# A hybrid decoder layer on one core: the products with x by a 2x2 recursion of seven products, ahead of everything else

## The chip, the cores and the metric

The kernel runs on one core of a Trainium2 chip. The metric is device time of one execution in microseconds (us). The engines named below are TensorE (PE in the profile; its weight loads are shown as PEld), VectorE (DVE), ScalarE (ACT), GpSimd (POOL) and SyncE (SP), whose queue issues all transfers.

## The reference

One decoder layer is applied to a prompt of 1024 tokens and to eight decode tokens, which have caches of their own. Both groups share the weights; the kernel puts them side by side as T = 1032 columns. D is 1024. Everything is float32.

```python
z = x @ w_in                                # [T, 7680], the single combined projection
xr, yr, q, k, v, xq, g = jnp.split(z, SPLIT_IDX, axis=-1)   # 1024, 1024, 1024, 256, 256, 1024, 3*1024
xc, conv_new = causal_conv(xr, conv_buf, conv_w, conv_b)    # width 4
hs, h_new = rg_lru(xc, h0, ...)             # h_t = a_t h_(t-1) + u_t; a, u from two block-diagonal products
a_out = hs * gelu(yr)
s_out = swa_prompt(q, k, v, sinks)          # window 128, 16 query heads, 4 key heads of 64; swa_decode for decode tokens
c_out = mem_attn(xq, mem_k, mem_v)          # 256 memory tokens, 4 heads of 256
gates = sigmoid(g + b_gates)                # three gates
merged = sum(gates[n] * (branch_n @ w_branch[n]))
h = layer_norm(ALPHA * x + merged @ w_out)
gt, up = split(h @ w_gate_up)               # 2 * 2816
h = layer_norm(ALPHA * h + (silu(gt) * up) @ w_down)
```

The prompt's memory keys and values come from `mem_prompt @ w_mem_kv`; the decode tokens read theirs from caches (`cmk`, `cmvT`), and local keys and values too (`cwk`, `cwvT`). New cache contents and states are outputs as well.

## The kernel before

Activations lie transposed: features on 128 partitions, tokens along the row. The 1032 tokens are cut into chunks of 384, 384 and 264 (`CH`). A product of two float32 matrices is made of three single-pass products: each operand is split into a high and a low part (`split`: ACT writes the rounded copy, L58, and DVE subtracts it, L59), and `mm3` (L79) adds high×high, high×low and low×high in PSUM (L84 to L86). A tile of 128 output features (`mm_tile`, L88) runs over eight blocks of the contraction for each chunk, so it is 72 matmuls. Weights come by `weights` (L72): one transfer of 512 KB into one of two raw buffers and a split. `load_branch` (L97) brings a branch's output back from DRAM and splits it.

The framework fixes one order of instructions for each engine ahead of time, so each engine works strictly in order and a waiting instruction holds up all that stand behind it on its engine. All transfers are issued by SP in one queue. `issue_after` puts a piece of work behind a given instruction in that order.

The stages in order:

1. `mem_attention` (L242). x is loaded and split into resident operands. For each of four heads: the query products of two feature tiles (`xq`), the memory's keys and values (`mem_kv`, L155: `mk`, `mv`), then scores, softmax, transposes and the weighted sum (`mem_head`, L202: `cs`, `cp`, `cpt`, `co`), whose result goes to DRAM. `dec_mem` (L578) does the decode tokens' attention into their own memories on DVE: query rows go through DRAM and are broadcast (`dcq`), keys come by two buffers (`dck`), DVE multiplies and adds up (`dcj`, L593), PE transposes the scores (`dct`), and the same follows with values (`dcv`, `dcpb`, `dcw`, L616).
2. `win_attention` (L406). Value products (`win_kv`), key products (`win_keys`), query products (`win_queries`) and 32 blocks of local attention (`win_block`, L350), 4 key heads by 8 blocks of 128 queries. A block has score matmuls (`bs`), a masked maximum (L371), exponentials (L377), a normalization that is shared by DVE (L386) and POOL (L384), transposes with a split (`bt`, `bph`, `bpl`), the product with the values (`bo`) and the sum of its two halves (L402). The products for the next key head stand between blocks.
3. `lru` (L541). For each of eight feature tiles the product `xr`, the convolution, the gate products, the recurrence (a scan on DVE, L524) and, from `yr`, the gelu; the result stays in SBUF as split operands.
4. `merge` (L706). For branch a, then c, then s: gate products (`ga`, `gc`, `gs`) two tiles ahead, and branch products (`bra`, `brc`, `brs`). The decode tokens' local attention (`dec_win`, scores with `dsk`, `dsq`, `dsj`, L655; softmax; values with `dsv`, `dspb`, `dsw`, L700) is put one token at a time behind these products.
5. `out_proj` and `ffn` (L893, L930) with the two layer norms.

So 58 feature tiles of x @ w_in and the values (216 matmuls with 256 columns) are spread over stages 1 to 4.

Of the kernel before, what the change touches and what calls it, by code (L numbers as in the profile page):

```python
# [2 lines left out]

# [4 lines left out]
F32 = mybir.dt.float32  # L8
# [21 lines left out]
DEC_VALUES = ((), (), (), (0,1), (2,), (3,), (4, 5), (6, 7))  # L30
YR_AFTER = ((2,), (3,), (4,), (5,), (6,), (), (), (7,))
# [10 lines left out]
class Builder:  # L42
# [6 lines left out]
    # ---------------------------------------------------------------- helpers  # L49
    def slot(self, kind, c, name, n=None):  # L50
        return self.slots.tile([P, n or CH[c][1]], F32R, tag=f"{kind}{c}", name=name)
# [4 lines left out]
    def split(self, hi, lo, src):  # L56
        """hi + lo = src exactly, in the operand format of the tensor engine's single-pass float32."""
        ins = self.nc.scalar.copy(hi, src).ins  # L58
        self.nc.vector.tensor_sub(lo, src, hi.bitcast(F32))  # L59
        return ins  # L60
# [18 lines left out]
    def mm3(self, ps, terms, closes=True):  # L79
        """ps = sum over terms of stationary^T moving, each operand as (hi, lo)."""  # L80
        nc = self.nc
        last = len(terms) - 1
        for i, ((sh, sl), (mh, ml)) in enumerate(terms):
            nc.tensor.matmul(ps, sh, mh, start=i == 0, stop=False)  # L84
            nc.tensor.matmul(ps, sh, ml, start=False, stop=False)  # L85
            self.last_mm = nc.tensor.matmul(ps, sl, mh, start=False, stop=closes and i == last).ins  # L86

    def mm_tile(self, w, act, c, name, tag="mm", nk=KT):  # L88
        """[128 features, tokens of chunk c] = w^T act, w = (hi, lo) of an m-tile, act[k][c] = (hi, lo)."""
# [7 lines left out]
    def load_branch(self, src, name):  # L97
        """a branch's output from DRAM, [128, 8, T]: act[k][c] = (hi, lo)."""
# [10 lines left out]
    # ---------------------------------------------------------------- phases  # L109
    def setup(self):  # L110
        nc, ctx, tc, io = self.nc, self.ctx, self.tc, self.io
        self.cst = ctx.enter_context(tc.tile_pool(name="cst", bufs=1))
        self.slots = ctx.enter_context(tc.tile_pool(name="slots", bufs=16))
        self.wpool = ctx.enter_context(tc.tile_pool(name="wpool", bufs=3))
# [5 lines left out]
        self.mask = self.cst.tile([P, 256], F32, name="mask")  # L120
# [6 lines left out]
    def load_consts(self):  # L127
        nc, io = self.nc, self.io
        nc.sync.dma_start(self.vec, io["vec"])
        nc.sync.dma_start(self.ident, io["cst"][:, 0:P])  # L130
        nc.sync.dma_start(self.mask, io["cst"][:, P:P + 256])

    def load_x(self, c):
        """x of chunk c, staged through what will hold queries."""
        t0, n = CH[c]
        for k in range(0, KT, 2):
            raw = self.ph.tile([P, TP], F32, tag="cq", name=f"xr{k}_{c}", bufs=6)[:, :2 * n]
            raw = raw.rearrange("p (k t) -> p k t", k=2)
            self.x_loaded = self.nc.sync.dma_start(raw, self.io["xT"][:, k:k + 2, t0:t0 + n]).ins
            for j in range(2):  # L140
                hi, lo = self.slot("H", c, f"xh{k + j}_{c}"), self.slot("L", c, f"xl{k + j}_{c}")
                self.split(hi, lo, raw[:, j, :])
                self.x[k + j][c] = (hi, lo)

    def load_mem(self):
        nc, io = self.nc, self.io
        self.memx = []
        for k in range(KT):
            hi, lo = self.slot("H", 0, f"memh{k}", NM), self.slot("L", 0, f"meml{k}", NM)
# [5 lines left out]
    def mem_kv(self, h):  # L155
        """keys of head h by feature, values by memory token."""
        nc, io = self.nc, self.io
        mk, mv = [], []
        for m in (2 * h, 2 * h + 1):
# [8 lines left out]
            hi, lo = self.slot("H", 1, f"mkh{m}", NM), self.slot("L", 1, f"mkl{m}", NM)  # L168
# [3 lines left out]
        for tt in range(2):  # L172
# [9 lines left out]
            hi, lo = self.slot("H", 2, f"mvh{h}_{tt}", 256), self.slot("L", 2, f"mvl{h}_{tt}", 256)  # L182
# [3 lines left out]

    def dec_query(self, ps, qd, m, scale):
        """keeps the scaled query of the decode tokens, [128 features, 8]."""
        self.nc.scalar.mul(qd[:, m * NB:(m + 1) * NB], ps[:, 256:264], scale)

    def mem_query(self, w, q, m, c):
        t0, n = CH[c]
        ps = self.mm_tile(w, self.x, c, f"xq{m}_{c}")
        n = min(n, TP - t0)
        self.split_scaled(q[0][:, t0:t0 + n], q[1][:, t0:t0 + n], ps[:, :n], 1.0 / 16.0)
        if c == 2:
            self.dec_query(ps, self.qdc, m, 1.0 / 16.0)

    def mem_query_tiles(self, m):
        return tuple(self.ph.tile([P, TP], F32R, tag="cq", name=f"cq{e}{m}", bufs=6) for e in "hl")  # L200
# [41 lines left out]
    def mem_attention(self):  # L242
        nc, io = self.nc, self.io
        self.qdc = self.cst.tile([P, KT * NB], F32, name="qdc")
        self.x = [[None] * 3 for _ in range(KT)]
        w = [self.weights(io["win"][28], D, "wxq0")]
        self.load_x(0)
        w.append(self.weights(io["win"][29], D, "wxq1"))
        self.load_x(1)
        self.load_mem()  # L250
        self.load_x(2)
        with self.tc.issue_after(self.x_loaded):
            self.load_consts()
        q = [self.mem_query_tiles(m) for m in range(2)]
        for c in range(3):
            for m in range(2):
                self.mem_query(w[m], q[m], m, c)
        self.lru_consts()
        for h in range(4):
            mk, mv = self.mem_kv(h)  # L260
            self.mem_head(h, q, mk, mv)
            if h < 3:
                q = []
                for m in (2 * h + 2, 2 * h + 3):
                    w = self.weights(io["win"][28 + m], D, f"wxq{m}")
                    q.append(self.mem_query_tiles(m))
                    for c in range(3):
                        self.mem_query(w, q[-1], m, c)
            with self.tc.issue_after(self.x_loaded):
                self.dec_mem(h)  # L270
        nc.sync.dma_start(self.scr["c"][:, :, TP:T], self.cdec)

    def win_kv(self):
        """keys as stacks [hi; hi] and [lo; lo] per kv head, values as [hi | lo] per block."""
        nc, io = self.nc, self.io
        self.kd = self.cst.tile([P, 2 * NB], F32, name="kd")
        self.vd = self.cst.tile([NB, 256], F32, name="vd")
        self.vs = []
        w = [self.weights(io["wv"][j], D, f"wv{j}") for j in range(2)]
        for blk in range(9):  # L280
            c, off = min(blk // 3, 2), (blk - 3 * min(blk // 3, 2)) * P
            nt = P if blk < 8 else NB
            ps = self.bank("mm", f"v{blk}")[:nt, :256]
            self.mm3(ps, [
                ((self.x[k][c][0][:, off:off + nt], self.x[k][c][1][:, off:off + nt]),
                 (w[k // 4][0][:, (k % 4) * 256:(k % 4 + 1) * 256], w[k // 4][1][:, (k % 4) * 256:(k % 4 + 1) * 256]))
                for k in range(KT)
            ])
            if blk == 8:
                nc.scalar.copy(self.vd, ps)  # L290
                break
            if blk == 7:
                vraw = self.sm.tile([P, 256], F32, tag="kvraw", name="pwv", bufs=1)
                nc.scalar.copy(vraw, ps)
                nc.sync.dma_start(io["o_pwv"], vraw)
            pair = []
            for half in range(2):
                kind = "H" if blk % 2 == 0 else "L"
                v = self.slots.tile([P, 256], F32R, tag=f"{kind}{half}", name=f"vs{blk}_{half}")
                v3 = v.rearrange("p (g e d) -> p g e d", g=2, e=2)  # L300
                src = ps[:, half * P:(half + 1) * P].rearrange("p (g d) -> p g d", g=2)
                nc.scalar.copy(v3[:, :, 0, :], src)
                nc.vector.tensor_sub(v3[:, :, 1, :], src, v3[:, :, 0, :].bitcast(F32))
                pair.append(v)
            self.vs.append(pair)
        self.ks = {}

    def win_keys(self, m):
        nc, io = self.nc, self.io
        w = self.weights(io["win"][24 + m], D, f"wk{m}")  # L310
        kk = [[self.ph.tile([P, TP], F32R, tag="ks", name=f"ks{m}_{g}_{e}", bufs=5) for e in range(2)]
              for g in range(2)]
        for c, (t0, n) in enumerate(CH):
            ps = self.mm_tile(w, self.x, c, f"k{m}_{c}")
            n = min(n, TP - t0)
            for g in range(2):
                src = ps[g * 64:(g + 1) * 64, :n]
                own = kk[g][0][g * 64:(g + 1) * 64, t0:t0 + n]
                for e in range(2):
                    nc.scalar.copy(kk[g][0][e * 64:(e + 1) * 64, t0:t0 + n], src)  # L320
                for e in range(2):
                    nc.vector.tensor_sub(kk[g][1][e * 64:(e + 1) * 64, t0:t0 + n], src, own.bitcast(F32))
            if c == 2:
# [792 lines left out]
```

## Time and profile before

Three runs took 2108.48, 2110.21 and 2118.28 us: median 2110.21 us.

| | |
|---|---|
| profiled execution, time and span | 2110.1 us |
| PE busy | 2039.2 us (97%) |
| PE weight loads busy | 1992.5 us (94%) |
| DVE busy | 1067.1 us (51%) |
| ACT busy | 755.0 us (36%) |
| POOL busy | 99.0 us (5%) |
| moved by transfers | 166.90 MB, 79 GB/s over the span |

Busy time is the time in which an engine had an instruction under way; a matmul that waits for its clock or for its operand inside the pipeline counts as busy too. The granted clock is the TensorE clock as a share of full speed. In a group's row stand the count, the sum, the mean length of one in ns, and then the idle time of the engine just before them with what ended it.

### The profile page before, as it was taken

The page shows a single profiled execution, that of the slowest core. Times are in us where ns is not written, and L with a number is a line of the kernel's source. Part 1 is how long each engine was busy: PE and PEld are TensorE (multiplying, and loading weights), DVE is VectorE, ACT ScalarE, POOL GpSimd, SP SyncE. Part 2 cuts the span into 40 slices and gives each one's busy share as a digit, 9 for nine tenths or more (in the row PEclk, how much of TensorE's full clock was granted, in tenths as well). Part 3 has the DMA queues.
Part 4 walks back from the last instruction along what each step waited for, and adds up shares of the span by engine and source line. Part 5 has one row for each costly group of instructions (what it writes and reads, how often), then busy time and mean ns, then how long its engine had stood idle before and what let it go on. Part 6 is the DMA issues. An engine that isn't in the chain of part 4 may idle for free.

```text
span 2110.1 us, 32562 instructions
## 1 busy us (share of the span) xinstructions
PE 2039.2 (97%) x13013; PEld 1992.5 (94%) x13013; DVE 1067.1 (51%) x2434; ACT 755.0 (36%) x1574; POOL 99.0 (5%) x167
## 2 busy tenths in 40 slices
PE   8998889999999999999999999999999999999997
PEld 8988888889899999999999999899999999999996
DVE  6455569998777643423442257832322322223357
ACT  6333347777766521311131144522201221112134
POOL 0000001111211100000000001200000000000001
PEclk9999999999999999999999999999999999999999
DMA  6366641112111122422441123011111111111112
GB/s 228 128 188 196 185 121 41 47 36 56 46 43 46 48 94 81 154 78 88 126 131 41 50 85 101 17 60 41 50 50 41 51 50 44 47 42 59 38 53 81
DMA packets 100855, 166.90 MB, mean 79 GB/s; under 512 B 12112, under 2 KB 69696, under 8 KB 100672
## 3 DMA queue, kind: packets, MB, share of 16 engines
q1 hardware_dynamic: 100704, 164.82, 24.9%
q8 instruction: 102, 1.67, 0.3%
q14 instruction: 49, 0.40, 0.1%
HBM read 149.41 MB, written 17.45 MB: 79 GB/s over the span
## 4 chain that ended last, share of the span: by engine, by line
PE 79%; DVE 10%; DMA 5%; ACT 3%; issue 2%; POOL 1%; SPq 0%; ACTq 0%; DVEq 0%; POOLq 0%
PE fg L84 4%; PE fg L86 4%; PE fg L85 4%; PE fu L84 4%; PE fu L86 4%; PE fu L85 4%; PE d L86 3%; PE d L85 3%; PE d L84 3%; DMA dck<-cmk 2%; PE brc L86 1%; PE brs L84 1%; PE gs L84 1%; PE gc L84 1%; PE gc L86 1%
## 5 line engine op out<-in xcount | busy, mean ns | idle before, releaser
L84 PE MATMUL fg<-hh,wfg_h 128*128 128x384 f32 (+1 forms) x528 | 168.4, 319 | 2.9 <-DVE acc L912 1.7
L85 PE MATMUL fg<-hl,wfg_h 128*128 128x384 f32 (+1 forms) x528 | 167.8, 318 | 0.7 <-DVE hl L923 0.7
L84 PE MATMUL fu<-hh,wfu_h 128*128 128x384 f32 (+1 forms) x528 | 167.6, 317 | 0.5 <-ACT wfu_h L58 0.5
L85 PE MATMUL fu<-hl,wfu_h 128*128 128x384 f32 (+1 forms) x528 | 167.6, 317 | 0.0
L86 PE MATMUL fu<-hh,wfu_l 128*128 128x384 f32 (+1 forms) x528 | 167.4, 317 | 0.0
L86 PE MATMUL fg<-hh,wfg_l 128*128 128x384 f32 (+1 forms) x528 | 167.4, 317 | 0.0
L86 PE MATMUL d<-gh,wd_l 128*128 128x384 f32 (+1 forms) x360 | 114.4, 318 | 0.0
L85 PE MATMUL d<-gl,wd_h 128*128 128x384 f32 (+1 forms) x360 | 114.3, 317 | 0.0
L84 PE MATMUL d<-gh,wd_h 128*128 128x384 f32 (+1 forms) x360 | 114.1, 317 | 0.0
L58 ACT CAST gh<-ft 128x384 fp32r<-128x384 f32 (+1 forms) x66 | 31.7, 481 | 224.8 <-DVE ft L941 224.8
L941 DVE TENSOR_TENSOR ft<-ft,fu 128x384 f32<-128x384 f32 (+1 forms) x66 | 33.8, 512 | 152.8 <-PE fu L86 152.7
L84 PEld LDWEIGHTS fg<-hh,wfg_h 128*128 128x128 f32 x528 | 99.1, 188 | 3.9 <-DVE acc L912 2.0
L85 PEld LDWEIGHTS fg<-hl,wfg_h 128*128 128x128 f32 x528 | 99.2, 188 | 1.3 <-DVE hl L923 1.1
L84 PEld LDWEIGHTS fu<-hh,wfu_h 128*128 128x128 f32 x528 | 99.1, 188 | 0.8 <-ACT wfu_h L58 0.8
L86 PEld LDWEIGHTS fg<-hh,wfg_l 128*128 128x128 f32 x528 | 99.4, 188 | 0.0
L85 PEld LDWEIGHTS fu<-hl,wfu_h 128*128 128x128 f32 x528 | 99.2, 188 | 0.0
L86 PEld LDWEIGHTS fu<-hh,wfu_l 128*128 128x128 f32 x528 | 99.1, 188 | 0.0
L939 DVE SCALAR_TENSOR_TENSOR ft<-ft,fg 128x384 f32<-128x384 f32 (+1 forms) x66 | 33.8, 512 | 124.2 <-ACT ft L938 123.4
L961 DVE SCALAR_TENSOR_TENSOR acc<-d,acc 128x384 f32<-128x384 f32 (+1 forms) x48 | 24.8, 516 | 126.0 <-PE d L86 126.0
L84 PE MATMUL xq<-xh,wxq_h 128*128 128x384 f32 (+1 forms) x192 | 64.1, 334 | 6.1 <-ACT xh L58 6.1
L84 PEld LDWEIGHTS d<-gh,wd_h 128*128 128x128 f32 x360 | 67.7, 188 | 0.0
L86 PEld LDWEIGHTS d<-gh,wd_l 128*128 128x128 f32 x360 | 67.6, 188 | 0.0
(568 smaller groups left out, 6327.7 us busy)
## 6 DMA issues: line engine op xcount, KB each, us to landing
wfg_r<-wgu SPq DMA_DIRECT2D x22, 512.0 KB, 3.5
wfu_r<-wgu SPq DMA_DIRECT2D x22, 512.0 KB
dck<-cmk SPq DMA_DIRECT2D x32, 256.0 KB, 3.2
dcv<-cmvT SPq DMA_DIRECT2D x32, 256.0 KB, 3.5
wxq_r<-win SPq DMA_DIRECT2D x8, 512.0 KB, 3.8
wmk_r<-wmk SPq DMA_DIRECT2D x8, 512.0 KB, 4.5
wmv_r<-wmv SPq DMA_DIRECT2D x8, 512.0 KB
scr_c<-cob SPq DMA_DIRECT2D x16, 256.0 KB, 2.0
```

The costliest lines, as they stand in the source:

```text
L58: ins = self.nc.scalar.copy(hi, src).ins
L84: nc.tensor.matmul(ps, sh, mh, start=i == 0, stop=False)
L85: nc.tensor.matmul(ps, sh, ml, start=False, stop=False)
L86: self.last_mm = nc.tensor.matmul(ps, sl, mh, start=False, stop=closes and i == last).ins
L939: nc.vector.scalar_tensor_tensor(t, t, 1.0, pg, op0=ALU.add, op1=ALU.mult)
L941: nc.vector.tensor_mul(t, t, pu)
L961: nc.vector.scalar_tensor_tensor(a, ps, 0.5, a, op0=ALU.mult, op1=ALU.add)
```

## The change

All of x @ w_in is computed first, in a new stage `project`. Its 60 feature tiles are taken two at a time as 30 units. For a unit, the pair of feature tiles, the two halves of the contraction and the two halves of the tokens form a 2x2 by 2x2 product of blocks, which is done with seven block products instead of eight (Strassen's recursion in Winograd's form, one level). `combos` makes the seven combinations of x for each quarter of the tokens (258 columns), each split into two parts and kept for the whole stage. `fast_quarter` makes a unit's seven weight combinations (four sums, seven splits of 128x512), `fast_product` the twelve matmuls of a product (four blocks, three terms), `fast_step` combines them: the first ones are copied out of PSUM by ACT, others are added on DVE, two accumulate in place in PSUM.

The results leave as follows (`Finish`). Gates go through tanh to a DRAM scratch `g`. Memory queries, local queries and keys are scaled, split and stored (`spill`). Values are transposed by PE, split and stored (`v_rows`). The LRU (`lru`) and the decode tokens' memory attention (`dec_mem`) are now generators, which `pump` moves one step further after each product; the LRU's result goes to a scratch `a`.

After that `mem_attention` loads its queries from DRAM, and between its heads stands the decode tokens' local attention: four tokens' scores behind head 0 and four behind head 1 with the softmax, four tokens' values behind head 2 and four behind head 3. Then `windows` runs the 32 local blocks; from the fourth block on, one branch product (branch c, then a) stands behind every second block, and each product loads its gate from DRAM. One product of a and the eight of s follow. `out_proj` and `ffn` stay as they were. In a block, the part of the normalization that POOL did is done by ACT.

```diff
+HT = T // 2
+QN = T // 4
+UNITS = (
+    ("xq", 0), ("lru", 0), ("gate", 0), ("xq", 1), ("lru", 1), ("gate", 1), ("xq", 2), ("lru", 2), ("gate", 2),
+    ("xq", 3), ("lru", 3), ("gate", 3), ("k", 0), ("lru", 4), ("v", 0), ("q", 0), ("lru", 5), ("gate", 4),
+    ("q", 1), ("lru", 6), ("gate", 5), ("q", 2), ("lru", 7), ("gate", 6), ("q", 3), ("gate", 7), ("gate", 8),
+    ("gate", 9), ("gate", 10), ("gate", 11),
+)
...
+    def fast_quarter(self, st, i):
+
+        nc, (r0, r1), u = self.nc, st["raw"], st["u"]
+        h = D // 2
+        if i in (1, 2, 4, 5):
+            src = self.w1.tile([P, h], F32, tag="sum", name=f"us{u}_{i}", bufs=3)
+            a, b = {1: (r1[:, :h], r1[:, h:]), 2: (st.get(1), r0[:, :h]), 4: (r0[:, :h], r1[:, :h]),
+                    5: (st.get(2), r0[:, h:])}[i]
+            nc.vector.tensor_add(src, a, b)
+            st[i] = src
+        else:
+            src = {0: r0[:, :h], 3: r0[:, h:], 6: r1[:, h:]}[i]
+        hi = self.w1.tile([P, h], F32R, tag="qh", name=f"uh{u}_{i}", bufs=4)
+        lo = self.w1.tile([P, h], F32R, tag="ql", name=f"ul{u}_{i}", bufs=4)
+        self.split(hi, lo, src)
+        st["q", i] = hi, lo
+
+    def fast_product(self, st, i, p, ts, ps, opens):
+
+        nc = self.nc
+        sh, sl = st["q", i]
+        th, tl = ts[p][i]
+        mm = partial(nc.tensor.matmul, ps, skip_group_check=not opens)
+        for k in range(4):
+            w, x = slice(k * P, (k + 1) * P), slice(k * QN, (k + 1) * QN)
+            mm(sh[:, w], th[:, x], start=opens and k == 0, stop=False)
+            mm(sh[:, w], tl[:, x], start=False, stop=False)
+            self.last_mm = mm(sl[:, w], th[:, x], start=False, stop=k == 3).ins
...
+            self.fast_product(st, i, p, ts, ps, i in (0, 1, 3))
+            if i in (0, 1, 2):
+                st["s", i, p] = small(("p1s", "p5s", "u2s")[i], p)
+                nc.scalar.copy(st["s", i, p], ps)
+            elif i == 3:
+                nc.vector.tensor_add(st["za"][:, cols(0, p)], c, st["s", 0, p])
+            elif i == 4:
+                nc.vector.scalar_tensor_tensor(st["zb"][:, cols(1, p)], b, -1.0, st["s", 1, p], op0=ALU.mult,
+                                               op1=ALU.subtract)
+            elif i == 5:
+                nc.vector.tensor_add(st["za"][:, cols(1, p)], d, st["s", 2, p])
+            else:
+                finish.late(st["zb"][:, cols(0, p)], b)
...
+        load(0)
+        ts = [self.combos(p, self.x_quarter) for p in range(2)]
...
+        todo = [(u, i) for u in range(n) for i in range(7)]
+        ahead = 3
+        for u, i in todo[:ahead]:
+            self.fast_quarter(st[u], i)
+        for k, (u, i) in enumerate(todo):
+            if i == 1 and u + 1 < n:
+                load(u + 1)
+            if k + ahead < len(todo):
+                v, j = todo[k + ahead]
+                self.fast_quarter(st[v], j)
+            self.fast_step(st[u], i, ts, finish[u])
+            self.pump()
...
     def mem_attention(self):
...
+        self.load_mem()
+        self.dec_win()
         for h in range(4):
+            q = []
+            for m in (2 * h, 2 * h + 1):
+                pair = tuple(self.ph.tile([P, TP], F32R, tag="cq", name=f"cq{e}{m}", bufs=6) for e in "hl")
+                for e in range(2):
+                    nc.sync.dma_start(pair[e].bitcast(F32), self.scr["xq"][:, m, e, :])
+                q.append(pair)
             mk, mv = self.mem_kv(h)
             self.mem_head(h, q, mk, mv)
+            with self.tc.issue_after(self.last_load), self.tc.issue_after(self.last_mm), \
+                    self.tc.issue_after(self.last_split):
+                if h < 2:
+                    for b in range(4):
+                        self.dec_win_scores(4 * h + b)
+                    if h == 1:
+                        pr = self.dec_win_softmax(self.dec_win_turn())
+                        nc.sync.dma_start(self.dec_p.rearrange("b h k -> (b h) k"), pr)
+                else:
+                    for b in range(4):
+                        self.dec_win_values(4 * (h - 2) + b)
...
+    def windows(self):
...
+        for kv in range(4):
+            nxt = None
+            for b in range(8):
+                self.win_block(kv, ops, b)
+                if b == 4 and kv < 3:
+                    nxt = self.win_load(kv + 1)
+                if kv == 0 and b < 2:
+                    continue
+                if b % 2 and len(todo) > 2:
+                    br, m = todo.popleft()
+                    if m == 0:
+                        act = self.load_branch(self.scr[br], f"b{br}")
+                    self.product("ca".index(br), br, m, act)
+            ops = nxt
...
             if g % 2:
-                nc.gpsimd.tensor_scalar(pg[g], pg[g], r, 0.0, op0=ALU.mult, op1=ALU.add)
+                nc.scalar.mul(pg[g], pg[g], r)
...
+        with pool("tp", "right") as self.tp, pool("w1") as self.w1, pool("z") as self.z, pool("dp1") as self.dp:
+            self.project()
+        self.wpool = self.ctx.enter_context(pool("wpool"))
+        with pool("ph1") as self.ph, pool("dp2") as self.dp:
+            self.mem_attention()
```

631 lines of the change are left out of this document (306 added, 325 removed).

## The prediction

> **What bounds the kernel now.** I read the profile's first page, then busy time by stretch, then the TensorE (PE) timeline where nothing disturbs it, then the groups of instructions, the transfers and the chain of waits.
>
> ```profile
> span 2110.1 us, 32562 instructions
> ...
> PE 2039.2 (97%) x13013; PEld 1992.5 (94%) x13013; DVE 1067.1 (51%) x2434; ACT 755.0 (36%) x1574; POOL 99.0 (5%) x167
> ...
> PEclk9999999999999999999999999999999999999999
> DMA  6366641112111122422441123011111111111112
> ```
>
> PE is busy nearly always; DVE half the time. The sum is made against this execution (2110.1 us), which is also the median of the three runs (2110.21). I take 0.5% (2099.7 to 2120.8) as what can be told from no change.
>
> Stretches: start, memory attention (from 0), local attention, LRU, merge, and the rest. Columns: window, length, then busy time with count for PE, PEld, DVE, ACT, POOL, granted clock, DMA share, GB/s.
>
> ```profile
> 0.00:31.70 31.70, 25.02 (x144) 24.32 (x145) 23.32 (x72) 20.38 (x44) 1.36 (x12) 1.00 0.75 263
> 0.00:255.80 255.80, 229.91 (x1542) 216.99 (x1543) 142.34 (x432) 105.19 (x247) 1.36 (x12) 0.96 0.57 183
> 255.80:516.30 260.50, 247.99 (x1550) 224.60 (x1549) 221.17 (x731) 174.93 (x523) 30.64 (x64) 0.99 0.23 63
> 516.30:702.00 185.70, 175.69 (x1088) 171.14 (x1088) 141.84 (x194) 129.39 (x204) 30.73 (x43) 0.99 0.16 49
> 702.00:1249.30 547.30, 543.28 (x3474) 541.25 (x3473) 208.30 (x464) 131.45 (x220) 5.42 (x13) 1.00 0.28 87
> 1249.30:2110.10 860.80, 842.31 (x5368) 838.52 (x5366) 353.45 (x617) 214.02 (x381) 30.90 (x35) 0.99 0.17 55
> ```
>
> Busy time hides slow matmuls, so I price PE by its undisturbed pace (each row's start and length):
>
> ```profile
> 1559.72 0.29 PE L86 MATMUL d<-gh,wd_l 128*128 128x264 f32 x1
> ...
> 1561.55 0.29 PE L86 MATMUL d<-gh,wd_l 128*128 128x264 f32 x1
> 1561.67 0.33 PE L84 MATMUL d<-gh,wd_h 128*128 128x384 f32 x1
> ...
> 1567.91 0.33 PE L84 MATMUL d<-gh,wd_h 128*128 128x384 f32 x1
> ```
>
> Fifteen steps of 264 columns in 1.83 us are 122.0 ns each; 36 steps of 384 in 6.24 us are 173.3 ns. The line through both is 9.1 ns + 0.4275 ns per column: 119.4 ns at 258 columns, 118.6 at 256, 228 at 512, 64 at 128. An old feature tile (48 matmuls of 384, 24 of 264) is 11.25 us.
>
> With these paces memory attention needs 8×11.25 (xq) + 576×0.1186 + 96×0.228 + transposes 4 = 185, with 26 for the value products that this stretch also holds 211 of its 255.8 us: 45 lost. Local attention needs 217 of 260.5 (44 lost), LRU 170 of 185.7 (16), merge 541 of 547.3 (6).
>
> **The products with x.** Removed: 58 tiles × 11.25 = 652.5 us and 216 value matmuls × 0.1186 = 25.6, together 678. Added: 30 units × 7 products × 2 token quarters × 12 matmuls = 5040 × 0.1194 = 602. Saved: 76 us.
>
> The Trainium skill ("TensorE: Matmul & The Clock Gate", Back-to-back issue gap) gives sustained rates of about 81 ns at 128 columns and 131 at 512. Between them, as an estimate, 258 columns cost 98 ns and 384 cost 114: 494 us instead of 476, a loss of 18. The trace has 173.3 ns at 384, so it doesn't agree.
>
> What the seven products ask of DVE and ACT instead:
>
> ```profile
> L59 DVE TENSOR_TENSOR bpl<-bt,bph 128x512 fp32r<-128x512 f32 x60 | 41.0, 688 | 9.8 <-ACT bph L58 8.3
> L59 DVE TENSOR_TENSOR wfg_l<-wfg_r,wfg_h 128x1024 fp32r<-128x1024 f32 x22 | 26.9, 1225 | 24.6 <-PE fg L86 22.8 <-ACT wfg_h L58 1.8
> L59 DVE TENSOR_TENSOR gl<-ft,gh 128x264 fp32r<-128x264 f32 x22 | 9.4, 427 | 1.0 <-ACT gh L58 1.0
> L593 DVE SCALAR_TENSOR_TENSOR dcj<-dck,dcq 128x256 f32<-128x256 f32 x64 | 27.2, 424 | 32.0 <-DMA dck<-cmk 19.7 <-DMA dcq<-dcq 9.4 <-DVE mvl L59 1.6
> L616 DVE SCALAR_TENSOR_TENSOR dcw<-dcv,dcpb 128x256 f32<-128x256 f32 x64 | 27.0, 422 | 16.7 <-DMA dcv<-cmvT 14.7 <-DMA dcpb<-dcpd 1.1
> L524 DVE TENSOR_TENSOR_SCAN sq<-tr,ti 128x1024 f32<-128x1024 f32 x8 | 18.3, 2290 | 4.8 <-POOL tr L522 4.7
> L520 DVE SCALAR_TENSOR_TENSOR th<-tr,th 128x1032 f32<-128x1032 f32 x8 | 9.9, 1233 | 18.5 <-ACT sq L519 18.5
> ...
> 376.37 1.21 DVE L59 TENSOR_TENSOR wk_l<-wk_r,wk_h 128x1024 fp32r<-128x1024 f32 x1
> 377.50 0.15 DVE L379 TENSOR_TENSOR bst<-bst 128x4 f32<-128x4 f32 x1
> ```
>
> Back to back, DVE starts the next instruction some 85 ns before the last ends (1.13 us between starts, 1.21 long). So a unit's four sums and seven low parts (128×512) are 11 × 0.60, and its six PSUM combinations 6 × 0.34: 8.6 us of DVE for 20.1 of PE, covered. An LRU tile brings about 16 more (one scan of 2.29, about twelve of some 1.2). Units 1 to 12 take 241 us of PE; DVE there has 12 × 8.6 + 4 × 16 + the decode tokens' memory attention (128 × 0.42 + its softmax, 60) + spills of eight tiles (9) = 236. That leaves DVE without slack, and the memory attention's waits on transfers, 32.0 + 16.7 us above, aren't hidden by it: I take 44 of these 49 as PE time, for DVE is in order and each wait holds up the next quarter's low part. Bounds: 0 (the generator asks for one token per 2.9 us step, and two key buffers may be enough) and about 95 (waits doubled, as the queue now also carries the spills and gates).
>
> The start: fourteen split tiles and eight sums of 1032 columns are 22 × 1.14 = 25 us of DVE, and quarters another 12, while unit 0 is 20 us of PE. DVE begins at 7 to 9 us, so unit 0's last product starts no earlier than 44: about 25 us of hole, where before 9.2 of the first 31.7 were lost (144 matmuls are 22.5). LRU latency and ACT tables, 16 lost before, I put at 14. LRU's gate products and transposes remain at 24. The phase: 602 + 24 + 25 + 44 + 14 = 709.
>
> **Memory attention** now loads its queries from DRAM and holds the decode tokens' local attention in heads 0 to 3, where merge had covered it.
>
> ```profile
> 843.51 0.38 SPq L646 DMA_DIRECT2D dsk<-cwk  x1
> ...
> 849.87 0.43 DVE L655 TENSOR_TENSOR dsj<-dsq,dsk 128x256 f32<-128x256 f32 x1 [3.40 <-DMA dsk<-krow]
> ...
> 853.41 0.42 DVE L657 TENSOR_REDUCE dss<-dsj 128x4 f32<-128x256 f32 x1
> ...
> 1026.02 0.29 DVE L700 SCALAR_TENSOR_TENSOR dsw<-dsv,dspb 128x128 f32<-128x128 f32 x1 [0.36 <-DMA dspb<-dspd]
> ...
> 1028.66 0.08 DVE L700 DVE_READ_ACCUMULATOR dsw<-dsv,dspb 128x1 f32 x1
> ...
> 1032.47 0.29 DVE L700 SCALAR_TENSOR_TENSOR dsw<-dsv,dspb 128x128 f32<-128x128 f32 x1 [2.66 <-DMA dspb<-dspd]
> ...
> 1037.54 0.29 DVE L700 SCALAR_TENSOR_TENSOR dsw<-dsv,dspb 128x128 f32<-128x128 f32 x1
> ```
>
> A token's scores take 6.4 us from load to first product and 4 of DVE; with two buffers some 5 us each. Value tokens begin about 5.5 us apart (1026.02, 1032.47, 1037.54), of which 2.7 is DVE. In the changed instruction order DVE does tokens 3 to 7 and their softmax before it splits the weight tile that head 2's keys need. So PE, which needs 47 us for heads 0 and 1, waits for 8 × 5 + 28 (DVE's own work for two heads) + softmax and start 8 (an estimate) = 76, after a change of phase of 16 (the last gate store stands ahead of the first loads in the SP queue). Heads 2 and 3, with four value tokens of 5.5 us each, take 35 and 36: 163 in all against 97 of PE. Bounds for the waits: 25 if the tokens lie beside head work, 90 if every load waits for its predecessor.
>
> By the Trainium skill ("DMA: Bandwidth & Descriptors", Anatomy of one DMA) a transfer has some 2 us fixed, so the two dependent ones of a token would be 4.3 us and not 6.4: an estimate of 10 us less. The trace's 6.4 us decides.
>
> **Local attention with products.**
>
> ```profile
> L371 DVE CUSTOM_DVE_ANT_0 bp<-bs,mask,vec 128x256 f32<-128x256 f32 x112 | 51.0, 475 | 1.9 <-PE bs L368 0.9
> L386 DVE TENSOR_SCALAR bp<-bp,bst 128x256 f32<-128x256 f32 x56 | 22.9, 441 | 0.4
> L402 DVE TENSOR_TENSOR bob<-bo,bob 64x256 f32<-64x256 f32 x64 | 26.4, 413 | 6.9 <-ACT bob L401 6.1
> ...
> L377 ACT ACTIVATE bp<-bp,bst 128x256 f32<-128x256 f32 x112 | 55.9, 500 | 10.0 <-DVE bst L373 9.5
> L377 ACT ACTIVATION_READ_ACCUMULATOR bp<-bp,bst 128x1 f32 x128 | 24.1, 188 | 0.0
> ```
>
> A block is 8 × 0.1186 + 8 × 0.064 + 4 × 0.228 = about 2.2 us of PE and 5 of DVE and ACT. Two blocks with one product are 4.5 + 11.25 = 15.7 us of PE beside some 12 of DVE (10 for the blocks, 2 to 4 for the product, 1.1 for its weights, less overlap). That is covered, narrowly. The first four blocks have no product: 26 us. Then 28 × 2.2 + 15 × 11.25 = 231 and, for the two branch loads (24 splits each on DVE) and the narrow cover, 20: 277. The normalization moved from POOL to ACT is 2 × some 0.4 us per block on ACT (the estimate is from the exponential's 0.50 at the same size), which then has some 12 of each 15.7 (eight exponentials, four high parts, four copies, one weight tile): nothing. Nine products stay behind: 9 × 11.25 + 4 = 105.
>
> **The sum:** 709 + 163 + 277 + 105 + 861 (unchanged rest) = 2115; with the two attention terms rounded by a few us I say 2112. The 76 us saved by counting are eaten by decode work with no cover and by a change of phase.
>
> **Rivals.** Faster: the generators hide the memory decode. For it: DVE was busy 142 of 255.8 us when it waited, and a token per 2.9 us step isn't much. Against it: DVE's 236 of 241 us. Without the 44, with 10 less at the start and 8 less in memory attention: 2050. It decides from the point where waits cost under 30 us.
>
> Slower: the project phase is starved by DVE. If its waits cost 95 instead of 44, it is 760 and the whole 2163. For it: one more cause (a busier SP queue, a buffer of z not free) is enough, as DVE has no slack. Against it: after unit 12 DVE is loose again.
>
> The narrow products don't pay: at 678 / 5040 = 134.5 ns the saving is nil and the time 2112 + 76 = 2188. For it only slow matmuls after waits, seen at
>
> ```profile
> 110.42 0.42 PE L85 MATMUL xq<-xl,wxq_h 128*128 128x264 f32 x1
> 110.64 0.42 PE L86 MATMUL xq<-xh,wxq_l 128*128 128x264 f32 x1
> ```
>
> (264 columns 0.22 us apart, not 0.122), in a stretch whose clock was 0.96.
>
> The Trainium skill (same page on TensorE, Why this matters for your kernels) says that PE gaps of more than about 3 us lower the clock; the 0.96 agrees in sign.
>
> **How the numbers follow.** The forecast 0.50 (own range 2080 to 2145), faster 0.20, starved 0.25, narrow 0.05. Faster by over 0.5%: 0.20 + 0.15 of the forecast's lower part = 0.35; within: 0.20; slower: 0.15 + 0.25 + 0.05 = 0.45. The range goes from 2055 (half of the faster case left out) to 2185 (the narrow case and a little more left out).
>
> **What would show it.** Project at 709 us, with 258-column matmuls at 119 ns apart where nothing waits; DVE waiting on memory keys and values in units 1 to 12; PE idle at head 2's keys on the low part of their weights, released by DVE behind the decode scores; local attention near 277. The prediction is wrong if project ends before 670 or after 750, or if head 2's keys start without a gap.

## The result and the profile after

The changed kernel takes 2145.89 us (median of four runs, 2144.73 to 2147.10) against 2112.98 for the kernel before in the same comparison: a ratio of 1.0161, with a 95% interval of 1.0140 to 1.0182. It is slower by some 33 us. The prediction said 2112, within a range of 2055 to 2185, and gave "slower by over 0.5%" the largest chance (0.45).

The first page of the profile after, as far as it answers to the lines shown of before:

```profile
span 2144.1 us, 34798 instructions
...
PE 1993.4 (93%) x13679; PEld 1944.0 (91%) x13679; DVE 1247.7 (58%) x2764; ACT 867.1 (40%) x1834; POOL 71.3 (3%) x95
...
PE   6999999999997856599998999999999999999997
...
PEclk9999999999998979799999999999999999999999
DMA  5665552333334566864632423011121111111112
```

PE is busy for less time than before (1993.4 us, 2039.2 before), and yet the span is 34 us longer. The holes are in slices 13 to 17 of 40, which is about 670 to 900 us, and there the granted clock falls too. The busy time of the stretches says the same (columns as in the prediction: window, length, PE, PEld, DVE, ACT, POOL, clock, DMA share, GB/s). The projections end at 672.3, the first local block begins at 871.3, `out_proj` at 1274.6:

```profile
0.00:46.00 46.00, 29.34 (x174) 26.90 (x175) 38.86 (x64) 23.80 (x36) 4.12 (x12) 0.93 0.52 172
46.00:295.00 249.00, 237.73 (x1928) 235.77 (x1927) 208.98 (x521) 133.20 (x257) 9.61 (x17) 0.99 0.60 195
295.00:672.30 377.30, 377.30 (x3120) 377.22 (x3121) 265.58 (x435) 212.21 (x400) 25.07 (x23) 1.00 0.33 116
...
672.30:871.30 199.00, 119.15 (x753) 101.36 (x750) 110.39 (x332) 73.27 (x177) 1.70 (x8) 0.82 0.70 221
871.30:1162.00 290.70, 274.20 (x1698) 251.70 (x1699) 210.11 (x687) 179.97 (x528) 0.00 (x0) 0.97 0.50 140
1162.00:1274.60 112.60, 104.40 (x648) 103.67 (x647) 60.14 (x113) 30.86 (x58) 0.00 (x0) 0.97 0.35 118
1274.60:2144.10 869.50, 851.23 (x5368) 847.42 (x5366) 353.61 (x617) 213.78 (x381) 30.81 (x35) 0.99 0.17 54
```

Against the prediction's terms:

| stretch | forecast | measured | difference |
|---|---|---|---|
| projections | 709 | 672.3 | -37 |
| memory attention, up to the first local block | 163 | 199.0 | +36 |
| local attention, products, to `out_proj` | 277 + 105 | 403.3 | +21 |
| `out_proj` and `ffn`, unchanged code | 861 | 869.5 | +9 |
| sum | 2115 | 2144.1 | +29 |

So a sum that was only 1.4% off is made of four errors, and the two largest, -37 and +36, cancelled each other. What PE waited for in memory attention, from the table of waits for 672 to 872 us (what waited, what it waited for, total us, count, longest):

```profile
PE mk L93 <- ACT wmk_h L67: 20.3, 4, 9.2
PE dst L772 <- DVE dss L764: 17.5, 1, 17.5
PE bs L471 <- DMA st<-scr_q: 15.0, 1, 15.0
PE drt_s L679 <- ACT drow_s L680: 8.7, 3, 6.8
```

`mk` are the memory keys, which wait for the high part of their weights, `dst` is the transpose of the decode tokens' scores, `bs` the first score matmul of local attention, and `drt_s` are the transposes that turn the tokens' queries into rows. All four rows are waits behind small work or loads, and PE is busy for only 60% of the stretch. The order in the SP queue and on PE shows how they hang together; first SP's rows, then PE's (start, length, and in brackets the idle time before):

```profile
770.54 0.50 SPq L754 DMA_DIRECT2D dsk<-krow  x1
...
772.67 1.20 SPq L78 DMA_DIRECT2D wmk_r<-wmk  x2
...
777.99 0.45 PE L772 MATMUL dst<-ident,dss 128*128 128x128 f32 x1 [17.45 <-DVE dss L764]
781.28 0.58 PE L93 MATMUL mk<-memh,wmk_h 128*128 128x256 f32 x1 [2.85 <-ACT wmk_h L67]
...
782.54 0.58 PE L95 MATMUL mk<-memh,wmk_l 128*128 128x256 f32 x1 [0.47 <-DVE wmk_l L68]
...
783.14 0.42 PE L94 MATMUL mk<-meml,wmk_h 128*128 128x256 f32 x1
783.35 0.41 PE L95 MATMUL mk<-memh,wmk_l 128*128 128x256 f32 x1
```

The weights of head 2's keys are issued behind the last decode token's key, and on PE the keys stand behind `dst`. After the wait the keys' matmuls come 0.21 us apart, where the prediction counts 0.1186.

One row of the table of stretches was not to be expected at all: the last stages run the same code as before and take 8.7 us more. The PE timeline shows a slower pace. In this window of the changed kernel a tile has 48 matmuls of 384 columns in a row; these are the first and the last:

```profile
1589.79 0.34 PE L93 MATMUL d<-gh,wd_h 128*128 128x384 f32 x1
...
1598.10 0.34 PE L95 MATMUL d<-gh,wd_l 128*128 128x384 f32 x1
```

47 steps in 8.31 us are 176.8 ns, where the prediction's rows had 173.3.

### The profile page after: what moved, and what is told of

Same layout as the page of the kernel before. It is cut to its first block, busy times and chain, and to the rows that moved or that the text cites. A ratio compares the mean times of both kernels' runs of the same rounds, so it can differ in the third digit from the quotient of the medians.

```text
span 2144.1 us, 34798 instructions
## 1 busy us (share of the span) xinstructions
PE 1993.4 (93%) x13679; PEld 1944.0 (91%) x13679; DVE 1247.7 (58%) x2764; ACT 867.1 (40%) x1834; POOL 71.3 (3%) x95
## 4 chain that ended last, share of the span: by engine, by line
PE 54%; DVE 4%; DMA 2%; ACT 2%; issue 0%; SPq 0%; ACTq 0%; DVEq 0%
PE fg L93 4%; PE fg L94 4%; PE fg L95 4%; PE fu L93 4%; PE fu L95 4%; PE fu L94 4%; PE d L93 3%; PE d L94 3%; PE d L95 3%; PE brs L93 1%; PE brc L95 1%; PE brs L94 1%; PE brs L95 1%; PE brc L94 1%; PE brc L93 1%; PE bra L95 1%
## 5 line engine op out<-in xcount | busy, mean ns | idle before, releaser
L211 PE MATMUL ub<-th,uh 128*128 128x258 f32 x960 | 274.8, 286 | 14.4 <-ACT th L67 10.9
L212 PE MATMUL ub<-tl,uh 128*128 128x258 f32 x960 | 272.8, 284 | 2.4 <-DVE tl L68 2.4
L213 PE MATMUL ub<-th,ul 128*128 128x258 f32 x960 | 274.1, 286 | 0.7 <-DVE ul L68 0.7
L211 PEld LDWEIGHTS ub<-th,uh 128*128 128x128 f32 x960 | 183.1, 191 | 16.0 <-ACT th L67 11.4
L212 PEld LDWEIGHTS ub<-tl,uh 128*128 128x128 f32 x960 | 183.6, 191 | 2.9 <-DVE tl L68 2.9
L213 PEld LDWEIGHTS ub<-th,ul 128*128 128x128 f32 x960 | 183.2, 191 | 1.2 <-DVE ul L68 1.2
L211 PE MATMUL ud<-th,uh 128*128 128x258 f32 x480 | 137.6, 287 | 2.0 <-ACT th L67 2.0
L212 PE MATMUL ud<-tl,uh 128*128 128x258 f32 x480 | 136.2, 284 | 0.0
L213 PE MATMUL ud<-th,ul 128*128 128x258 f32 x480 | 136.0, 284 | 0.1
L67 ACT CAST uh<-us 128x512 fp32r<-128x512 f32 x120 | 74.5, 621 | 124.2 <-PE ud L212 43.5
```

The source lines that it names most:

```text
L211: mm(sh[:, w], th[:, x], start=opens and k == 0, stop=False)
L212: mm(sh[:, w], tl[:, x], start=False, stop=False)
L213: self.last_mm = mm(sl[:, w], th[:, x], start=False, stop=k == 3).ins
```

## The experiments

Theory after the result: the recursion saves what the count says; what it saves is lost in memory attention, where the decode tokens' local attention makes PE wait; 10 to 15 us more are lost to where the operand slots lie. Rivals: the recursion's DVE work eats its saving; the waits come from the order of loads whatever stands between; the slower pace is a matter of power or clock.

**Seven products or eight.** The edit replaces the seven combinations by the four blocks of x and of the weights:

```diff
-        keep(b11, 0)
-        t1 = self.zt(f"t1_{p}")
...
+        for i, src in enumerate((b11, b21, b12, b22)):
+            keep(src, i)
...
-        todo = [(u, i) for u in range(n) for i in range(7)]
+        todo = [(u, i) for u in range(n) for i in range(8)]
```

> The changed kernel with the plain eight block products per unit in place of seven: no weight sums, four weight quarters split per unit instead of seven, each result block summed in PSUM and copied out; all else, order of units and side work too, as in the changed kernel. 5760 matmuls of 258 columns instead of 5040. Theory: PE bounds the projections, so the recursion's saving arrives nearly whole there: 720 x 0.12 us = 86 us more, less some 10 to 20 for a shorter start and a loose DVE; projections 672 -> 735 to 750, the whole 2205 to 2225. Rival: DVE and ACT (which the recursion loads) bound the projections as much as PE; then they grow by 40 or less and the whole stays under 2190.

It took 2220.59 us, a ratio of 1.0519 (1.0501 to 1.0536) to the kernel before. The projections of this kernel by the windows view:

```profile
0.00:745.70 745.70, 725.27 (x5940) 723.23 (x5940) 355.74 (x734) 291.45 (x475) 33.63 (x52) 1.00 0.41 137
```

745.7 us against 672.3 with seven products: 73 us of the 86 that 720 matmuls of 0.12 us cost. DVE has 356 us there, where the recursion had 513 (39 + 209 + 266 in the rows above). So the recursion asks for 158 us more of DVE, and its saving falls only 13 us short of the count. The theory holds; the rival (growth under 40) falls.

**The decode tokens' memory attention**, left out of the projections:

```diff
-            if self.kind == "xq":
-                b.side[1].append(b.dec_mem(j))
...
+        nc.vector.memset(self.cdec, 0.0)
```

> The changed kernel without the decode tokens' attention into their memories (left out; zeros are stored in its place). The prediction charged 44 us of PE time in units 1 to 12 to its waits on transfers: then the projections fall from 672 to about 630 and the whole to about 2100. Rival: the generator, one token per step, hides them all but for the transposes that wait for DVE; then projections fall by 8 to 20, to 652 to 664, the whole to 2126 to 2138.

2126.62 us, ratio 1.0076 (1.0061 to 1.0092). The projections end at 655.2, 17 us earlier. The same stretch as in the second row of the changed kernel's table:

```profile
46.00:295.00 249.00, 248.76 (x2054) 248.56 (x2053) 180.04 (x295) 139.16 (x264) 19.32 (x17) 1.00 0.31 111
```

Without the tokens PE does 2054 matmuls in these 249 us, with them 1928. They cost 17 us in all, not 44: the rival. The changed kernel's trace says how much DVE waits for the tokens' loads during the projections. These are the rows of the same two multiplications that the prediction shows of before, with the idle time and its causes at the end:

```profile
L722 DVE SCALAR_TENSOR_TENSOR dcw<-dcv,dcpb 128x256 f32<-128x256 f32 x64 | 27.0, 421 | 19.9 <-DMA dcv<-cmvT 14.3 <-DMA dcpb<-dcpd 3.2 <-issue 1.9
L698 DVE SCALAR_TENSOR_TENSOR dcj<-dck,dcq 128x256 f32<-128x256 f32 x64 | 26.8, 418 | 4.6 <-DMA dck<-cmk 3.6 <-DMA dcq<-dcq 0.7
```

The waits for values are as long as before (19.9 us, 16.7 before), those for keys are nearly gone (4.6, 32.0 before): 24.5 us in all, half of the 49.

**The decode tokens' local attention**, left out of memory attention:

```diff
-                if h < 2:
-                    for b in range(4):
-                        self.dec_win_scores(4 * h + b)
...
+                if h == 3:
+                    nc.vector.memset(self.dec_out, 0.0)
+                    nc.sync.dma_start(self.scr["s"][:, :, TP:T], self.dec_out)
```

> The changed kernel without the decode tokens' local attention (scores, softmax and values are left out, zeros are stored; the cache outputs stay). Theory: these tokens are what makes PE wait in memory attention, on DVE and in the SP queue; without them the stretch from the end of the projections to the first local block falls from 199 to about 130 us and the whole by 60 to 75, to 2070 to 2085. Rival: the waits come from the order of weight loads and result stores in the SP queue, with or without the tokens; then the stretch stays over 170 us and the whole over 2115.

2079.12 us, ratio 0.9858 (0.9834 to 0.9881): 67 us less than the changed kernel, as the theory had it. From the end of the projections to the first local block:

```profile
669.90:826.20 156.30, 123.15 (x817) 109.13 (x815) 72.44 (x144) 77.13 (x185) 0.00 (x0) 0.91 0.71 228
```

156 us and not the 130 expected. This stretch now holds the first branch product too (72 matmuls, from 795 on, among those of head 3), but these are some 11 us, so the expectation was missed by about 15. The kernel before does the tokens' work and this one doesn't, so the ratio is no gain; it says that the tokens cost 67 us where they stand, twice what the change loses. Of the longest wait for queries at the first local block, 6.3 us of 15.0 stay without them.

**Their order alone.** Head 2's and head 3's key weights are loaded and split ahead of the tokens, and the transpose of the scores goes behind head 2:

```diff
             self.mem_head(h, q, mk, mv)
+            if h in (1, 2):
+                first = [self.weights(self.io["wmk"][m], D, f"wmk{m}") for m in (2 * h + 2, 2 * h + 3)]
...
-                    if h == 1:
+                else:
+                    if h == 2:
                         pr = self.dec_win_softmax(self.dec_win_turn())
```

> The changed kernel with the weights of the next head's keys loaded and split ahead of the decode tokens of heads 1 and 2, and the transpose of the decode scores (with the softmax) put behind head 2, so that PE has head 2's keys ahead of it. No work is left out. Theory: the 17.5 us that PE waits at that transpose, with head 2's keys behind it, and part of the 20 us at the keys' weights come from this order; the stretch of memory attention falls from 199 to 165 to 180, the whole by 15 to 30. Rival: the tokens' transfers and DVE work are a chain that ends last whatever stands ahead of it, so the wait moves to the values or the first local block; the whole changes by less than 8.

2137.01 us, ratio 1.0136 (1.0121 to 1.0151): some 9 us less by the medians, 5 by the ratios. The wait at `dst` is gone and another stands in its place (table of waits):

```profile
PE cs L93 <- ACT mkh L67: 29.8, 2, 27.6
```

`cs` are the scores of a head, which now wait for the high part of the keys. The first local block begins at 856.6 instead of 871.3. The theory's numbers were not met (the stretch takes 185 us), and the rival is the nearer: the wait moved. That the tokens would hold up PE here in any order is not shown by one other order.

**The same work beside the projections.** The tokens' scores, softmax and values become a generator that runs beside the last five units (their broadcast rows get two buffers instead of three):

```diff
+            if self.kind == "q" and j == 3:
+                b.side[1].append(b.dec_win_steps())
...
+    def dec_win_steps(self):
+        self.dec_win()
+        yield
+        for b in range(NB):
+            self.dec_win_scores(b)
+            yield
+        pr = self.dec_win_softmax(self.dec_win_turn())
...
```

> The changed kernel with the decode tokens' local attention made one more step generator that runs beside the last five units of the projections, where DVE has slack, and none of it left in memory attention. Theory: DVE (266 of 377 us busy after unit 12) takes in 8 x 3.4 + 8 x 2.7 = 49 us without holding up PE by more than 10; the memory attention stretch is as short as without these tokens, the whole 2080 to 2100. Rival: DVE waits on transfers hold up the weight splits there as they did in memory attention, and the projections grow by 40 or more; then the whole stays above 2125.

2109.76 us, ratio 1.0006 (0.9995 to 1.0016): no different from the kernel before, 36 us better than the changed one by the medians. The projections grew by 31 us, to 703.1, between the two expectations. Half of it is at one place on PE:

```profile
640.92 0.28 PE L213 MATMUL ub<-th,ul 128*128 128x258 f32 x1
647.19 0.47 PE L774 MATMUL dst<-ident,dss 128*128 128x128 f32 x1 [5.99 <-DVE dss L766]
...
657.63 0.58 PE L211 MATMUL ub<-th,uh 128*128 128x258 f32 x1 [3.12 <-DVE zb L240]
658.01 0.42 PE L212 MATMUL ub<-tl,uh 128*128 128x258 f32 x1
658.23 0.42 PE L213 MATMUL ub<-th,ul 128*128 128x258 f32 x1
```

The transpose stands right behind the last score in PE's order and waits 6.0 us for it. Behind it come nine gate products of the LRU, and then the next matmul of a unit, which waits another 3.1 us for DVE. So 16.7 us pass between two matmuls of the units, and after that they come 0.22 us apart instead of 0.12 for a while. The Trainium skill ("TensorE: Matmul & The Clock Gate", Why this matters for your kernels) says that idle gaps of more than about 3 us bring the clock to half; the 6 us gap and the 0.22 us agree.

**The place of the slots.** In the changed kernel the 384-column operand slots begin 480 bytes above a multiple of 512, before the change 128 above; the weights begin 128 above in both, except where they lie in such slots themselves (`out_proj` and the last part of `ffn`). Four runs move them. Two are of the changed kernel, with 96 and with 32 bytes set aside (slots at 384 and 448), two of the kernel before (slots at 224 with weights at 256, and slots at 480 with weights at 128):

```diff
-        with pool("acc") as self.acc:
+        with pool("pad", "right") as pad, pool("acc") as self.acc:
+            nc.vector.memset(pad.tile([P, 24], F32, name="pad"), 0.0)
```

> The changed kernel with 96 bytes per partition set aside, so that the operand slots of the last stages begin at multiples of 128 bytes as before the change (they lie at 96 above one in the changed kernel); nothing else differs. Theory: where an operand begins sets the pace of the 384-column matmuls (176.7 ns in the changed kernel's last stage, 173.4 before). Then the pace goes back to 173.4, the unchanged last stage (out_proj and ffn) from 869.5 to about 861 us, and the whole is 4720 x 3.3 ns = 15 us shorter, about 2130. Rival: the slower pace is a matter of the chip's power or clock after the preceding stages; then 2146 stays.

> The changed kernel with 32 bytes per partition set aside instead of 96, so that slots begin at 64 above a multiple of 128. If what slows the 384-column matmuls is a begin that isn't at a multiple of 64 bytes, the pace is 173.5 ns here as with 96, the whole about 2136; if it needs a multiple of 128, it is near 176.7, the whole 2146. (The kernel before, moved by 96 bytes, begins at 96 above too and kept 173.5 ns, so a third thing must take part in either case.)

> The kernel before the change with its operand slots moved by 96 bytes per partition (weights stay at multiples of 128); nothing else differs. Theory of alignment: its 384-column matmuls go from 173.4 to about 176.7 ns, 7600 x 3.3 ns = 25 us more, about 2138. Rival: no change, 2113.

> The kernel before the change with its operand slots at 480 above a multiple of 512 bytes, exactly as in the changed kernel, and weights at 128 above, also as there. If that place alone slows the 384-column matmuls, they go from 173.4 to 176.7 ns and the whole by 7600 x 3.3 ns = 25 us to about 2136. If not (2111 stays), the slowing needs something else of the changed kernel's layout, and stays open.

| kernel | slots, above a multiple of 512 | ratio to the kernel before (95%) | ns per 384 columns |
|---|---|---|---|
| changed | 480 | 1.0161 (1.0140 to 1.0182) | 176.8 |
| changed, 96 bytes | 384 | 1.0125 (1.0105 to 1.0146) | 174.0 |
| changed, 32 bytes | 448 | 1.0093 (1.0078 to 1.0108) | 173.4 |
| before, 96 bytes | 224 | 1.0006 (0.9993 to 1.0019) | 173.6 |
| before, as in the changed | 480 | 1.0096 (1.0079 to 1.0113) | 176.8 |

The pace in each row is worked out from the first and last of 48 matmuls of one tile, as above. First the kernel before with its slots at 480, then the changed kernel with 32 bytes:

```profile
1567.37 0.34 PE L84 MATMUL d<-gh,wd_h 128*128 128x384 f32 x1
...
1575.68 0.34 PE L86 MATMUL d<-gh,wd_l 128*128 128x384 f32 x1
```

```profile
1581.31 0.34 PE L93 MATMUL d<-gh,wd_h 128*128 128x384 f32 x1
...
1589.46 0.34 PE L95 MATMUL d<-gh,wd_l 128*128 128x384 f32 x1
```

8.31 us and 8.15 us for 47 steps. The place alone makes the kernel before slower by 20 us and the changed one by 8 to 15, and with the slots moved its last stage takes what it took before:

```profile
1273.80:2135.00 861.20, 842.91 (x5368) 839.01 (x5366) 353.79 (x617) 214.00 (x381) 30.88 (x35) 0.99 0.17 54
```

That is the run with 96 bytes. My rule for it, multiples of 64 or 128, is wrong: 224 is a multiple of neither and is fast. Power and clock fall as the cause.

The slots' place is not the whole of it. In `out_proj` of the changed kernel the weights lie in slots as well, so weights and moving operand both begin at 480. These are the first and the last of 24 matmuls of its first tile:

```profile
1274.64 0.34 PE L93 MATMUL op<-mh,wo0h 128*128 128x384 f32 x1
...
1278.63 0.33 PE L95 MATMUL op<-mh,wo0l 128*128 128x384 f32 x1
```

23 steps in 3.99 us are 173.5 ns: the fast pace, at the same place of the slots. So the slow pace goes with slots at 480 and weights at 128 together. In the last stages 2832 of the 3568 matmuls of 384 columns have both; at some 3 ns each that is 8.5 us of the 8.7 that were lost there. The 4720 of the expectation count all of them. No run moves the weights alone.

**Three edits together** (the third was not run by itself): slots at 384 as above; the generator beside the last seven units, with four steps between the last score and its transpose; and the first weights of memory attention ahead of the memory tokens, which get buffers of their own:

```diff
-                raw = self.raw(io["memT"][:, k * NM:(k + 4) * NM], 4 * NM, f"mem{k}")
+                raw = self.ph.tile([P, 4 * NM], F32, tag="memr", name=f"memr{k}", bufs=2)
+                nc.sync.dma_start(raw, io["memT"][:, k * NM:(k + 4) * NM])
...
+        for _ in range(4):
+            yield
         pr = self.dec_win_softmax(self.dec_win_turn())
...
+        first = [self.weights(self.io["wmk"][0], D, "wmk0")]
         self.load_mem()
```

> The changed kernel with three edits: the slots begin at multiples of 128 bytes; the decode tokens' local attention runs as a step generator beside the last seven units (the last query unit stands two places earlier), with four steps between the last score and the transpose of the scores; memory attention loads its first weights ahead of the memory tokens, which no longer occupy the weights' raw buffers. Theory: each gives what it gave alone and the early decode no longer stalls PE: projections under 690, memory attention as short as without the tokens, about 2146 - 10 - 60 - 5 = 2070 (2060 to 2085), under the kernel before the change. Rival: DVE or the SP queue has no room in the last units at all; then the projections stay near 703 and the whole near 2100.

2078.96 us, ratio 0.9844 (0.9827 to 0.9861): 1.6% faster than the kernel before, and within what was expected. Its stretches: projections, memory attention up to the first branch product, from there to `out_proj`, the rest:

```profile
0.00:690.30 690.30, 652.85 (x5233) 643.42 (x5233) 548.62 (x1217) 370.14 (x702) 46.58 (x60) 0.99 0.49 166
690.30:799.00 108.70, 94.92 (x672) 87.95 (x673) 60.54 (x116) 63.20 (x147) 0.00 (x0) 0.95 0.77 260
799.00:1214.80 415.80, 388.55 (x2411) 364.15 (x2410) 275.93 (x817) 217.06 (x606) 0.00 (x0) 0.96 0.45 134
1214.80:2075.80 861.00, 842.74 (x5368) 838.98 (x5366) 353.32 (x616) 213.86 (x381) 30.78 (x35) 0.99 0.17 54
```

From the end of the projections to `out_proj` it takes 524.5 us where the changed kernel took 602.3, and the projections pay 18 us for it. The first key product begins 8.6 us after the projections' end (698.9), not 17.9 (690.2 in the changed kernel).

## Why the prediction was right, and where its steps were not

**The products with x.** Right. The forecast was 602 us by pace; in the stretch after unit 12, 377.3 us hold 3120 matmuls with PE busy throughout. Seven products against eight gave 73 us of the 86. The estimate from the Trainium skill's rates ("TensorE: Matmul & The Clock Gate", Back-to-back issue gap), by which narrow products would have lost 18 us, isn't borne out: 120 ns at 258 columns here, not 98.

**The start.** Right: the first 46 us hold 174 matmuls, 20.8 us at 119.4 ns, so 25 us are lost, as forecast.

**Waits in units 1 to 12.** The failing step is "I take 44 of these 49 as PE time, for DVE is in order". Leaving the tokens out gave 17. Half of the 49 us didn't arise: DVE waited 24.5 us for the tokens' loads here, nearly all of it for values, so "DVE waiting on memory keys and values" came out for values and hardly for keys. The 17 us also hold the tokens' own DVE work and transposes, so PE paid for only a part of these waits. That split quarters in reserve (three steps ahead) hid the rest is likely, but no run changes the reserve. The 14 us for LRU latency and tables weren't seen either: PE is busy for all of 377.3 us after unit 12, and for 248.76 of 249 us before it when the tokens are left out. These two terms, 27 and 14 us too high, make up the -37 and a little more. The phase ended at 672.3 us, 2 us above the 670 below which the prediction called itself wrong. The rival "faster" had this condition right (under 30), and was still the wrong case, since it also took 10 us off the start, which came as forecast, and 8 off memory attention, which grew.

**Memory attention.** The mechanism was right and its size too small: 199 us, not 163. Above PE's own 97 that is 102 us, where 66 were forecast. PE is idle for 80 of them (199.0 less 119.15 busy), within the upper bound of 90 for the waits; 62 stand in the four rows above. The other 22 or so are matmuls that take longer: the step took the full clock for granted, and the row says 0.82. Head 2's keys were to wait for the decode scores, and they did, but not at the place that was named, the low part of their weights (0.47 us): PE stands at `dst`, 17.5 us, and then 2.9 us at the high part, whose load is behind the tokens' in the SP queue. What the step left out is the far end: the last tokens' loads and result stand ahead of the local attention's loads in the SP queue, and the first block waits 15.0 us for its queries (6.3 without the tokens). These are SP's rows for the tokens' result and the queries:

```profile
858.05 0.58 SPq L810 DMA_DIRECT2D scr_s<-dso  x1
...
863.28 6.07 SPq L449 DMA_DIRECT2D st<-scr_q  x8
```

The section of the Trainium skill that the prediction cites for 2 us per transfer ("DMA: Bandwidth & Descriptors", Anatomy of one DMA) is on transfers that GpSimd issues, and all of these are issued by SP; the trace's 6.4 us, by which the prediction went, is the only price measured here.

**Local attention.** Mis-sized by 21 us of 382. The blocks ahead of the first branch product were taken as 26 us and took 31 (871.3 to 902.6), at a clock of 0.80 as the windows view has it:

```profile
871.00:905.00 34.00, 21.60 (x97) 15.67 (x97) 23.94 (x93) 23.58 (x77) 0.00 (x0) 0.80 0.76 199
```

The slots' place costs 1152 x 3.3 ns = 4 us of the 24 products. The prediction's own terms for a block, 0.95, 0.51 and 0.91 us, add up to 2.37 and not to 2.2, which is 5 us for 28 blocks. And the first products of branch s wait 8.2 us in all, for their operand and behind DVE, which the sum doesn't have (table of waits for 871 to 1275 us):

```profile
PE brs L93 <- ACT bsh L67: 6.4, 1, 6.4
...
PE brs L93 <- DVE gts L551: 1.8, 1, 1.8
```

These four come to 22 us. That ACT takes over POOL's normalization for nothing was not tested on its own.

**The rest.** "861 (unchanged rest)" failed by 8.7 us, although no instruction changed: the pools moved the slots to 480, while most weights stayed at 128.

Of the cases, the outcome (2145.89) lies at the upper edge of the forecast's own range (2145), and by its number nearer to the "starved" rival (2163) than to 2112. By its mechanism it is the forecast: decode work without cover in memory attention eats the saving. The "starved" rival put the loss into the projections, which took 672 us and not 760. That the total came within 1.6% of 2112 is luck in part: the projections were priced too high by as much as memory attention was priced too low.

## What to carry to other kernels

Of a saving of 86 us counted in matmuls 73 arrived, even with 158 us more work on DVE beside it; what decided was where small, latency-bound work lay that the old order had covered. When a change moves stages, list such work first (decode tokens, transposes, one-row loads), and give it a place beside the longest stretch of PE work, one step at a time, with its transposes some steps behind what they need. And compare operand addresses of the code that did not change.

## What was not expected of the hardware

A matmul whose 384-column float32 operand begins 480 bytes above a multiple of 512, and whose weights begin 128 above, takes 176.8 ns instead of 173.4 to 174.0 with the operand at 128, 224, 384 or 448. In the kernel before this alone is 20 us. With the weights at 480 too it takes 173.5 ns, in the same run. The Trainium skill ("SBUF — State Buffer", Operand start alignment) allows every start at a multiple of the element size, which all of these are, and says that the runs behind it timed nothing. No run here tells what in the memory makes the pair of 480 and 128 slow.
